# First block's mixers: where the convolution taps are emitted, and the order of the output projection's units

## The chip, the cores and the metric

One core of one Trainium2 chip. The metric is the time of one execution on the device in microseconds; several executions are timed, and their median counts. A profile of one execution gives the start and the length of every instruction on the engines: PE (TensorE; PEld is its weight load), DVE (VectorE), ACT (ScalarE), POOL (GpSimd) and the DMA queue of SP (SyncE).

## What is computed

Two transformer blocks over 256 tokens of width 1024. The first has two layers, and the change lies in the mixer of each of them:

```python
proj = h @ w_in + b_in                       # columns: conv | q | k | v | memory query
conv_out = silu(layer_norm(depthwise_conv31(a * sigmoid(gate)) + conv_b))     # 256 channels
diff_out = rms(softmax(s1) @ v - lam * softmax(s2) @ v)                       # 4 heads, 512 wide
mem_out  = softmax(qm @ km.T) @ vm                                            # 4 heads, 256 wide
mixed = concatenate([conv_out, diff_out, mem_out]) @ w_out + b_out
x = layer_norm(ALPHA * x + mixed)
x = layer_norm(ALPHA * x + square(relu(x @ w_up)) @ w_down)
```

A second block (sparse attention, a state-space scan and a gated feed-forward) follows; the change does not touch it.

## The kernel before

All weights lie in HBM as units of 1 MB (128 partitions x 2048 floats). `weight` (L242 to L257) loads a unit with one DMA of SP's queue into a `raw` buffer, of which there are two, and splits it into a rounded part `hi` (ACT, L255) and a rest `lo` (DVE, L256), each in two halves; there are four buffers of `hi` and of `lo`. A raw buffer is free for the next unit's DMA when its `lo` is done. Each product is made of three matmuls, hi·hi, hi·lo and lo·hi (`mm3`, L261 to L263).

`mixer_ops` emits one layer's mixer for two token tiles t of 128 and two head pairs hp. First comes the convolution's input (`conv_in`, leaving `u`), then keys and queries (`chan`, two units each), the scores of the first head pair, the values, and the taps. `conv` is one chain of 31 steps for each of two channel halves c, on DVE, each step reading what the last one wrote:

```python
for j in range(1, 31):
    vec.scalar_tensor_tensor(out=y, in0=u[:, c, j:j + 256], scalar=tap(j), in1=y, op0=OP.mult, op1=OP.add)
```

Then a loop of four steps n goes over d = (0,0), (0,1), (1,0), (1,1), pairs (t, hp). Each step emits the scores of the next pair (`diff_scores`: matmuls L533, the reduction with the relative bias on DVE L540, four exponentials on ACT L519) and the values of this pair (`diff_values`: scaling on ACT L557 and DVE L558, transposes L340, eviction L561, matmuls L565). Step 0 also emits the memory query (`chan` "qm", one unit, 48 matmuls and eviction L495); steps 1 and 3 `diff_norm` (ACT L573 and L579); steps 1 and 2 `mem_attention` (matmuls L589, DVE L593, ACT L599 and L603); step 2 `mem_values` (transposes L615, eviction L617, matmuls L621, and a split into `mixT` at L345 and L346). Steps 0 and 1 emit `conv_out` (transposes L629, DVE L633 to L641, ACT L635 and L640). Parts of the second block's position bias, `position_bias_part`, are spread over the steps: loads `rel` through SP, ACT L877 and L882, matmuls L880.

The mixers' results lie side by side in `mixT`: columns 0 and 1 the convolution, 2 to 5 the four difference heads, 6 and 7 the memory. The output projection takes four units of two columns each, in the order of the list `order`: unit 0 is the convolution, 1 and 2 the difference heads, 3 the memory. In `layer`, `downs` (L279 to L291) adds them up in two accumulators `acc` (PSUM) for each token tile: for the units in front of the last both column halves c together, then the last unit. One unit of one token tile is 12 matmuls, so 48 a tile and 96 a layer. The accumulation makes their order fixed. `row` buffers, two in all, hold rows that are broadcast to all partitions: the convolution's norm (`self.cln`), then b_out, and the layer norm's gain and offset (ln_g, ln_b), loaded through SP (L369). Scores and memory scores use the same four `acc` buffers.

The order on each engine is not the order of the code. The tile framework puts the instructions into the engines' queues ahead of time, by its own estimate of when each is ready; among those that it holds ready, the one emitted first goes first. An instruction that is emitted late but needs little can therefore run early. Each engine then runs its queue strictly in that order.

Of the kernel before, what the change touches and what calls it, by code (L numbers as in the profile page):

```python
# [198 lines left out]
class Kernel:  # L199
# [455 lines left out]
    def mixer_ops(self, l):  # L655
        nc, vec, gp, a = self.nc, self.nc.vector, self.nc.gpsimd, self.a
        self.cln = self.row(a["lay"], 1536 * l)
        self.v = [self.b1.tile([128, 512], F32, name="v", tag=f"v{t}") for t in range(NT)]
        self.kT = self.new("kq", [128, 4, S])
        self.qT = self.new("kq", [128, 4, S])  # L660
        self.qmT = self.b1.tile([128, 2, S], F32, name="qmT")
        self.conv_in(l)
        eighth = lambda c: self.scaled[:, c:c + 1]
        self.chan(l, "k", 8, self.kT, lambda c: self.col("b_in", c), 1.0)
        self.chan(l, "q", 4, self.qT, eighth, 0.125)
        if l == 0:
            self.position_bias()
        self.mixT = self.pair("mh", [128, KD, S])
        d = [(0, 0), (0, 1), (1, 0), (1, 1)]
        st = self.diff_scores(l, 0, 0)  # L670
        vs = [self.weight("v", l, h) for h in range(2)]
        for t in range(NT):
            self.values(l, vs, t)
        self.conv(l, 0)
        self.conv(l, 1)
        for n, (t, hp) in enumerate(d):
            if n < 3:
                nxt = self.diff_scores(l, *d[n + 1])
            self.diff_values(l, t, hp, *st)
            st = nxt  # L680
            if n == 0:
                self.chan(l, "qm", 16, self.qmT, eighth, 0.125)
            if n < 2:
                self.conv_out(l, n)
            if n % 2:
                self.diff_norm(l, t)
            if 0 < n < 3:
                self.mem_attention(l, n - 1)
            if n == 2:
                self.mem_values(l)  # L690
            for m in range((0, 2, 3, 4)[n], (2, 3, 4, 8)[n]):
                self.position_bias_part(8 * l + m)
        bo = self.row(a["b_out"], D * l)
        for t in range(NT):
            vec.scalar_tensor_tensor(out=self.x[t], in0=self.x[t], scalar=ALPHA, in1=bo, op0=OP.mult, op1=OP.add)
        order = (0, 3, 1, 2)
        ws = [self.weight("out", l, i) for i in order]
        return order, ws

# [704 lines left out]
```

## Time and profile before

| | us |
|---|---|
| median of 3 runs | 1275.21 |
| lowest, highest | 1273.62, 1282.3 |
| profiled execution | 1279.33 |
| its span, first to last instruction | 1277.6 |

Times in rows are counted from the start of the span, so 1.73 us of the profiled execution lie outside of it. In a timeline row stand the start, the length, the engine, the line, the operation, what it writes and reads, the shapes and how many were merged; brackets give the idle time of the engine just before and what ended it. The mixer of the first layer runs from about 43 to 167 us, that of the second from about 360 to 476 us.

### The profile page before, as it was taken

To read this page: it belongs to the slowest core of one execution; us is meant where nothing else is said; L and a number is where in the kernel's file an instruction comes from. 1 tells how busy PE (TensorE), PEld (TensorE's weight loads), DVE (VectorE), ACT (ScalarE), POOL (GpSimd) and SP (SyncE) were. 2 spreads that over 40 slices of the span, in tenths; PEclk is the share of its full clock that TensorE was granted. 3 is DMA by queue.
4 is the path that set the end of the run, shared out by engine and by line. 5 is a ranking of instruction groups with operands and counts; after the bars stand their busy time and mean duration, and the time that the engine had idled before them with its cause. 6 is when DMAs were issued, how large, how long until landed. Compare 5 with 4: busy or idle time off the path is not lost.

```text
span 1277.6 us, 20408 instructions
## 1 busy us (share of the span) xinstructions
PE 1203.1 (94%) x8031; PEld 1064.6 (83%) x8031; DVE 966.1 (76%) x1741; ACT 662.8 (52%) x1082; POOL 65.2 (5%) x75
## 2 busy tenths in 40 slices
PE   6997989999999899999988899999999999999997
PEld 5886679899888568998877788789999968899996
DVE  5898577777789667787768995389999987655553
ACT  4546754444353875444335577555555634544441
POOL 2100000000000000000001000000111110000000
PEclk9998999999999899999989999999999999999999
DMA  8733567777561556777735344165454534554450
GB/s 310 263 138 122 191 217 261 253 294 278 198 239 67 190 189 242 273 272 256 279 105 192 120 161 167 70 243 190 164 185 185 185 110 159 198 199 180 183 198 33
DMA packets 53425, 247.81 MB, mean 194 GB/s; under 512 B 5277, under 2 KB 17597, under 8 KB 30545
## 3 DMA queue, kind: packets, MB, share of 16 engines
q1 hardware_dynamic: 52256, 243.22, 53.0%
q0 software_dynamic: 1072, 3.28, 0.8%
q8 instruction: 63, 1.03, 0.3%
q14 instruction: 34, 0.27, 0.1%
HBM read 241.06 MB, written 6.47 MB: 194 GB/s over the span
## 4 chain that ended last, share of the span: by engine, by line
PE 59%; DVE 18%; DMA 11%; ACT 7%; issue 4%; POOL 0%; SPq 0%; DVEq 0%; ACTq 0%; POOLq 0%
PE mm L263 11%; PE mm L262 11%; PE mm L261 11%; PE acc L263 7%; PE acc L261 7%; PE acc L262 6%; DVE lo L256 6%; DMA raw<-in_wts 6%; DVE cy L512 3%; DMA s<-in_ada 3%; ACT hi L255 3%; PE tr L340 1%; DVE t L779 1%; DMA rel<-reld 1%; DVE mask L1015 1%
## 5 line engine op out<-in xcount | busy, mean ns | idle before, releaser
L255 ACT ACTIVATE hi<-raw 128x1024 fp32r<-128x1024 f32 (+1 forms) x367 | 367.3, 1025 | 376.0 <-DMA raw<-in_wts 169.8
L256 DVE TENSOR_TENSOR lo<-raw,hi 128x1024 fp32r<-128x1024 f32 (+1 forms) x367 | 431.6, 1185 | 153.5 <-ACT hi L255 152.9
L261 PE MATMUL mm<-xT,hi 128*128 128x256 f32 x992 | 282.8, 285 | 2.6 <-DVE zs L1147 1.5
L263 PE MATMUL mm<-xT,lo 128*128 128x256 f32 x992 | 282.5, 285 | 0.0
L262 PE MATMUL mm<-xT,hi 128*128 128x256 f32 x992 | 282.1, 284 | 0.0
L261 PEld LDWEIGHTS mm<-xT,hi 128*128 128x128 f32 x992 | 191.8, 193 | 5.1 <-DVE zs L1147 1.7
L262 PEld LDWEIGHTS mm<-xT,hi 128*128 128x128 f32 x992 | 191.7, 193 | 0.8
L263 PEld LDWEIGHTS mm<-xT,lo 128*128 128x128 f32 x992 | 191.9, 193 | 0.2
L261 PE MATMUL acc<-hi,mh 128*128 128x512 f32 x320 | 127.8, 399 | 5.3 <-ACT mh L599 5.3
L262 PE MATMUL acc<-lo,mh 128*128 128x512 f32 x320 | 126.4, 395 | 0.0
L263 PE MATMUL acc<-hi,mh 128*128 128x512 f32 x320 | 125.9, 394 | 0.0
L262 PE MATMUL mm<-lo,xT 128*128 128x256 f32 (+1 forms) x288 | 85.7, 298 | 2.1 <-DVE lo L256 2.1
L263 PE MATMUL mm<-hi,xT 128*128 128x256 f32 (+1 forms) x288 | 86.4, 300 | 1.2 <-DVE xT L346 1.2
L261 PE MATMUL mm<-hi,xT 128*128 128x256 f32 (+1 forms) x288 | 87.1, 302 | 0.1
L779 DVE SCALAR_TENSOR_TENSOR t<-s,silu_c,t 128x512 f32<-128x512 f32 x84 | 62.9, 749 | 30.8 <-DMA s<-in_ada 30.3
L263 PE MATMUL mm<-h,lo 128*128 128x256 f32 x288 | 80.6, 280 | 0.0
L261 PE MATMUL mm<-h,hi 128*128 128x256 f32 x288 | 80.3, 279 | 0.0
L262 PE MATMUL mm<-h,hi 128*128 128x256 f32 x288 | 80.3, 279 | 0.0
L261 PEld LDWEIGHTS acc<-hi,mh 128*128 128x128 f32 x320 | 60.9, 190 | 18.7 <-ACT mh L599 6.1
L263 PEld LDWEIGHTS acc<-hi,mh 128*128 128x128 f32 x320 | 60.5, 189 | 13.8 <-issue 1.4
L262 PEld LDWEIGHTS acc<-lo,mh 128*128 128x128 f32 x320 | 60.7, 190 | 12.5 <-issue 1.1
L261 PEld LDWEIGHTS mm<-hi,xT 128*128 128x128 f32 x288 | 55.5, 193 | 5.2 <-issue 1.8
(382 smaller groups left out, 2220.7 us busy)
## 6 DMA issues: line engine op xcount, KB each, us to landing
raw<-in_wts SPq DMA_DIRECT2D x174, 1024.0 KB
s<-in_ada SPq DMA_DIRECT2D x48, 512.0 KB
rel<-reld SPq DMA_DIRECT2D x64, 64.0 KB
bias<-bo SPq DMA_DIRECT2D x16, 256.0 KB
bias<-bias SPq DMA_DIRECT2D x8, 512.0 KB
cr<-cumd SPq DMA_DIRECT2D x8, 512.0 KB
mh<-in_wts SPq DMA_DIRECT2D x3, 1024.0 KB
row<-in_ln_g SPq DMA_DIRECT2D x4, 512.0 KB
```

The costliest lines, as they stand in the source:

```text
L255: nc.scalar.activation(h[:, s], raw[:, s], AF.Copy)
L256: (lo_on or nc.vector).tensor_tensor(out=l[:, s], in0=raw[:, s], in1=h[:, s].bitcast(F32), op=OP.subtract)
L261: t.matmul(out=out, lhsT=l[0], rhs=r[0], start=start, stop=False)
L262: t.matmul(out=out, lhsT=l[0], rhs=r[1], start=False, stop=False)
L263: t.matmul(out=out, lhsT=l[1], rhs=r[0], start=False, stop=stop)
L340: self.nc.tensor.transpose(out=p[:, i, :], in_=x[:, i * 128:i * 128 + 128], identity=self.ident)
L512: vec.scalar_tensor_tensor(out=y, in0=u[:, c, j:j + 256], scalar=tap(j), in1=y, op0=OP.mult, op1=OP.add)
L779: vec.scalar_tensor_tensor(out=acc, in0=w[:, k, :], scalar=s, in1=acc, op0=OP.mult, op1=OP.add)
L1015: vec.scalar_tensor_tensor(out=isc, in0=rl[:, i, :], scalar=self.widx[:, t, h:h + 1], op0=OP.mult, op1=OP.add, in1=self.nadm[:, t, :] if h ...
```

## The change

The two calls of `conv` move from ahead of the loop into its steps 0 and 1, behind that step's `diff_values` (and in step 0 behind the memory query). `conv_out` moves from steps 0 and 1 to steps 2 and 3. The output projection adds memory, difference heads 0 and 1, convolution, difference heads 2 and 3, where it was convolution, memory, heads 0 and 1, heads 2 and 3. No instruction is added or removed.

```diff
         for t in range(NT):
             self.values(l, vs, t)
-        self.conv(l, 0)
-        self.conv(l, 1)
         for n, (t, hp) in enumerate(d):
             if n < 3:
                 nxt = self.diff_scores(l, *d[n + 1])
@@
             if n == 0:
                 self.chan(l, "qm", 16, self.qmT, eighth, 0.125)
             if n < 2:
-                self.conv_out(l, n)
+                self.conv(l, n)
+            else:
+                self.conv_out(l, n - 2)
             if n % 2:
                 self.diff_norm(l, t)
@@
-        order = (0, 3, 1, 2)
+        order = (3, 1, 0, 2)
         ws = [self.weight("out", l, i) for i in order]
```

## Rows read from the trace of the kernel before

**Rows 1.** The page: busy time, share of the span and number of instructions by engine; the chain that ended last, by engine.

```profile
PE 1203.1 (94%) x8031; PEld 1064.6 (83%) x8031; DVE 966.1 (76%) x1741; ACT 662.8 (52%) x1082; POOL 65.2 (5%) x75
PE 59%; DVE 18%; DMA 11%; ACT 7%; issue 4%; POOL 0%; SPq 0%; DVEq 0%; ACTq 0%; POOLq 0%
```

**Rows 2.** Busy time by stretch: the stretch, its length, then busy us (and instructions) of PE, PEld, DVE, ACT, POOL, the granted TensorE clock, the DMA engines' busy share, GB/s. Five stretches of the first layer, two of the second's mixer.

```profile
84.00:97.50 13.50, 11.99 (x56) 9.33 (x54) 13.22 (x50) 4.54 (x13) 0.00 (x0) 1.00 0.00 1
97.50:106.50 9.00, 4.57 (x31) 3.83 (x32) 9.00 (x32) 3.46 (x11) 0.74 (x3) 0.80 0.07 23
121.30:143.00 21.70, 18.14 (x104) 12.51 (x103) 9.50 (x30) 18.24 (x52) 1.57 (x2) 0.84 0.58 188
143.00:167.20 24.20, 22.83 (x133) 16.64 (x131) 17.75 (x30) 16.69 (x30) 2.01 (x2) 1.00 0.68 230
200.00:360.00 160.00, 159.99 (x991) 144.37 (x990) 126.72 (x159) 69.87 (x83) 0.92 (x1) 1.00 0.70 252
...
410.00:420.00 10.00, 9.94 (x78) 8.53 (x78) 10.00 (x27) 3.86 (x12) 0.55 (x1) 1.00 0.34 123
431.00:445.00 14.00, 10.14 (x49) 6.73 (x46) 6.74 (x25) 11.59 (x41) 1.56 (x2) 0.76 0.69 242
```

**Rows 3.** Timeline of DVE, first layer: the longest merged group of taps, the memory query's two `lo` halves, and the scaling of x by ALPHA, which is emitted behind the whole loop.

```profile
77.04 8.00 DVE L512 SCALAR_TENSOR_TENSOR cy<-u,cols,cy 128x256 f32<-128x256 f32 x20
...
102.26 2.35 DVE L256 TENSOR_TENSOR lo<-raw,hi 128x1024 fp32r<-128x1024 f32 x2
...
108.81 2.35 DVE L695 SCALAR_TENSOR_TENSOR x<-x,row 128x1024 f32<-128x1024 f32 x2
```

**Rows 4.** What SP's queue waited for (total us, times, longest us): the first row from 60 to 180 us, the second from 370 to 480 us. Then, from the timeline of SP in the first layer, the load of the layer norm's offset.

```profile
SPq L249 <- DVE lo L256: 42.9, 6, 27.1
...
SPq L249 <- DVE lo L256: 40.9, 6, 24.8
...
127.64 0.92 SPq L369 DMA_DIRECT2D row<-in_ln_b  x1
```

**Rows 5.** Timeline of PE, first layer: the waits behind the values, a group of value matmuls at full clock, and the wait ahead of the second token tile's first output unit.

```profile
102.02 0.41 PE L340 MATMUL tr<-ident,t 128*128 128x128 f32 x2 [2.69 <-DVE ds L517]
...
104.60 2.08 PE L565 MATMUL mm<-v,t 128*128 128x128 f32 x8 [1.73 <-ACT t L561]
...
118.58 1.16 PE L565 MATMUL mm<-v,t 128*128 128x128 f32 x8
...
128.35 0.79 PE L261 MATMUL acc<-hi,mh 128*128 128x512 f32 x1 [2.38 <-ACT mh L599]
```

**Rows 6.** The chain that ended last, first layer: start, length and kind of two of the memory query's matmuls, one before and one after the clock rose.

```profile
106.68 0.21 PE mm L261
...
113.55 0.12 PE mm L262
```

**Rows 7.** Timeline of ACT, first layer: the wait for the second pair's scores, the eviction of the memory query, and the rounding of the memory's result into `mixT`.

```profile
101.99 0.51 ACT L519 ACTIVATE s<-s,ds 128x256 f32<-128x256 f32 x1 [9.24 <-DVE ds L517]
...
113.83 0.84 ACT L495 ACTIVATE qmT<-mm,scaled 128x256 f32<-128x256 f32 x2 [1.82 <-PE mm L263]
...
142.02 0.60 ACT L345 ACTIVATE mh<-mm 128x512 fp32r<-128x512 f32 x1 [0.38 <-PE mm L621]
```

**Rows 8.** Groups by line and form (count, busy us, mean ns, idle before): taps from 85 to 105 us; exponentials with their sums, scalings and the rounding of the convolution's result from 113.8 to 142.7 us; exponentials with their sums from 419.7 to 452.7 us; from 121.3 to 142.9 us the output projection's hi·hi matmuls, one in three of its matmuls.

```profile
L512 DVE SCALAR_TENSOR_TENSOR cy<-u,cols,cy 128x256 f32<-128x256 f32 x26 | 11.0, 480 | 0.0
...
L519 ACT ACTIVATE s<-s,ds 128x256 f32<-128x256 f32 x4 | 2.0, 514 | 0.0
L557 ACT ACTIVATE t<-s,ds 128x256 f32<-128x256 f32 x4 | 1.8, 513 | 0.0
...
L519 ACT ACTIVATION_READ_ACCUMULATOR s<-s,ds 128x1 f32 x4 | 0.8, 208 | 0.0
L640 ACT ACTIVATE mh<-tr 128x256 fp32r<-128x256 f32 x2 | 0.8, 383 | 0.0
...
L519 ACT ACTIVATE s<-s,ds 128x256 f32<-128x256 f32 x8 | 4.0, 505 | 0.0
L519 ACT ACTIVATION_READ_ACCUMULATOR s<-s,ds 128x1 f32 x8 | 1.6, 199 | 0.0
...
L261 PE MATMUL acc<-hi,mh 128*128 128x512 f32 x8 | 4.3, 537 | 2.4 <-ACT mh L599 2.4
```

**Rows 9.** Timeline of PE, first layer: the first and the last of 24 output matmuls that follow each other without another instruction between them.

```profile
145.58 0.39 PE L262 MATMUL acc<-lo,mh 128*128 128x512 f32 x1
...
150.82 0.39 PE L261 MATMUL acc<-hi,mh 128*128 128x512 f32 x1
```

**Rows 10.** Timeline of ACT, second layer: the eviction of the first pair's transposes, the second pair's first exponential, the eviction of the memory query, and the rounding of the memory's result.

```profile
411.58 0.60 ACT L561 ACTIVATE t<-tr 128x512 f32<-128x512 f32 x1 [6.04 <-PE tr L340]
...
415.42 0.51 ACT L519 ACTIVATE s<-s,ds 128x256 f32<-128x256 f32 x1 [3.25 <-DVE ds L517]
...
419.73 0.84 ACT L495 ACTIVATE qmT<-mm,scaled 128x256 f32<-128x256 f32 x2
...
452.06 0.60 ACT L345 ACTIVATE mh<-mm 128x512 fp32r<-128x512 f32 x1 [0.50 <-PE mm L621]
```

**Rows 11.** Timeline of PE: the longest wait of the second layer's mixer, and the wait for the position bias ahead of the first layer's feed-forward.

```profile
438.68 0.80 PE L261 MATMUL acc<-hi,mh 128*128 128x512 f32 x1 [2.87 <-ACT mh L599]
...
172.27 0.52 PE L880 MATMUL tr<-step,bd 128*64 128x256 bf16 x6 [3.04 <-ACT step L877]
```

## The prediction

> **What bounds the kernel now.** The page first: PE is busy for 94% of the span and is 59% of the chain that ended last [rows 1], so time is won where PE waits or runs slowly. The stretches say where. In the feed-forward, from 200 to 360 us, PE is busy for 159.99 of 160 us; in the first layer's mixer, from 97.5 to 106.5 us, for 4.57 of 9, at a granted clock of 0.80, while DVE is busy throughout [rows 2]. So I read DVE's queue next. In the 20 us from 85 to 105 us, 26 taps take 11.0 us [rows 8], and behind them, at 102.26 us, stand the `lo` halves of the memory query's unit [rows 3]. Three engines wait for that. SP's queue waits 27.1 us on a `lo`, its longest [rows 4], and the DMA share falls to 0.00 [rows 2]. ACT waits 9.24 us for the second pair's scores, which DVE takes up only behind taps [rows 7]. PE waits 2.69 and 1.73 us, then does eight value matmuls in 2.08 us that take 1.16 us at full clock [rows 5], and the memory query's first matmuls at 0.21 us each, later ones at 0.12 [rows 6].
>
> From the memory query's eviction (113.83 us) to its attention's result in `mixT` (142.02 + 0.60 us) the bound is another one: ACT is busy for 18.24 of 21.7 us, PE has a clock of 0.84 [rows 2, 7]. PE gets through this with 24 of the 96 output matmuls, the convolution's: 8 of each of three kinds, of which the row shows one [rows 8]. From there PE is busy for 22.83 of 24.2 us to the end of the mixer [rows 2].
>
> The second layer has the same order but no hole at the same place: from 410 to 420 us PE is busy for 9.94 of 10 us [rows 2], though SP waits 24.8 us [rows 4] and ACT 6.04 and 3.25 us [rows 10]. Its loss lies from 431 to 445 us, PE 10.14 of 14 us at 0.76 [rows 2], the longest wait being 2.87 us for ACT's memory exponentials [rows 11].
>
> **What the planner will do.** Position in the code is a rank, not a time: the scaling of x, emitted behind the whole loop, ran at 108.81 us [rows 3]. Taps that fill DVE while keys and queries are made, such as the 20 from 77.04 us [rows 3], stay where they are, since nothing ahead of them in rank is ready. What moves are about 26 taps of the first layer, 11.0 us [rows 8], and about as many of the second: they fall behind the second pair's scores, the first pair's values and the memory query's `lo`. They need 11 us of DVE elsewhere, and there is room: from 121.3 to 143 us DVE works 9.5 of 21.7 us, from 431 to 445 us 6.74 of 14 [rows 2]. Their cost is then nothing; were that room gone, 11 us. Two chains of taps can still cut in between single DVE steps, one tap of 0.48 us at a time.
>
> **First layer, ahead of the memory query.** PE's waits of 2.69 + 1.73 = 4.4 us go [rows 5]. With them goes the slow clock behind them: 2.08 - 1.16 = 0.9 us on the value matmuls [rows 5], and on the query's 48 matmuls (113.83 - 106.68) - 48 x 0.12 = 1.4 us [rows 6, 7]. Sum 6.7 us. What is late next is PE itself, since the values fill it up to there.
>
> **Second layer, same place.** PE is full, so nothing: 0.
>
> **The stretch bound by ACT.** Exponentials that can run while ACT now waits leave it. First layer: the last pair's, 2.0 + 0.8 = 2.8 us; one of the two pairs of scalings, 1.8 / 2 = 0.9; and the rounding of the convolution's result, 0.8, which moves to its end [rows 8]. Sum 4.5 us. Second layer: two pairs' exponentials, 4.0 + 1.6 = 5.6 us [rows 8], and by the first layer's rows again 0.9 + 0.8: 7.3 us, of which the waits of 6.04 + 3.25 us can hold all [rows 10]. Unknown is how much other ACT work (rounding of output units, position bias) drops into the place; it may eat all of it (0), or the two gains may be as computed (11.8). I take the computed ones, being nearest to the waits seen.
>
> **The order of the units.** This speaks against the change. With the memory's unit first, no output matmul can run before the memory's result is there. The 24 that now fill the stretch come after it: 24 x (150.82 - 145.58) / 23 = 5.5 us a layer [rows 8, 9], as nothing covers them there. The convolution, third now, is wanted 24 matmuls, or 5.5 us, after the result, so the later taps and `conv_out` should not be waited for. Bounds for a wait on it: none, or the 2.69 us that a transpose waited for DVE [rows 5]; I take none.
>
> **Other queues.** The moved steps issue no DMA, but `conv_out` frees the row buffer of `cln`, into which ln_b goes, at 127.64 us now [rows 4]. Issued later, it holds back weight loads behind it in SP's queue; between nothing and the load's own 0.92 us a layer, and I take nothing, as the query's raw buffer comes free some 15 us earlier. POOL, 1.57 us busy of 21.7 [rows 2], takes `conv_out`'s small power without loss.
>
> **Sum.** First layer 6.7 + 4.5 - 5.5 = 5.7 us; second 7.3 - 5.5 = 1.8 us; together 7.5 us. The profiled execution, 1279.33 us, would become 1271.8; it lies 4.1 us over the median of the runs, so the median goes from 1275.2 to about **1268 us**. What follows, the feed-forward and the second block, is unchanged and should only shift.
>
> **Rivals.**
> *More is won.* The memory's result comes so early that PE never lacks work. Then every loss in the two mixers goes: 6.7 us, the 2.38 us wait [rows 5] and, with `rel` loads early in SP's queue, the 3.04 us for the position bias [rows 11], 12.1 us; and in the second layer 14 - 10.14 = 3.9 us [rows 2]. 16 us: 1259. For it: ACT's 9.24 us of waiting [rows 7] could hold three pairs. Against: the filler is gone.
>
> *Nothing moves in the stretch.* ACT stays as full as it is, with other work: 6.7 - 5.5 - 5.5 = -4.3 us, 1279.5. For it: ACT's busy share there is set by everything queued on it, not by scores alone.
>
> *Slower: the filler was worth more than its matmuls.* The place is PE between the memory query and the memory's result. Without the convolution's 24 matmuls PE waits longer for ACT, and the clock falls: after the waits of rows 5 it was 0.80, and the lost clock cost 0.9 + 1.4 = 2.3 us. If the memory's result comes less than 5.5 us earlier in both layers, this decides: 2 x (5.5 + 2.3) = 15.6 us lost, 1291. For it: from 431 to 445 us PE already lacks 3.9 of 14 us at a clock of 0.76 [rows 2]. Against: the 6.7 us ahead of it are nearly sure.
> [...]
>
> *The change doesn't do what it says.* The planner, holding the taps ready, still puts them ahead of the query's `lo`. Then only the order of the units acts: 2 x 5.5 = 11 us lost, 1286.
>
> **From cases to numbers.** Chances: forecast 0.42, more is won 0.23, nothing moves 0.18, slower 0.12, not as said 0.05. A measurement of this kernel can tell about 1%, 12.8 us, from no change. Faster than that (under 1262.5) are nearly all of the first rival and the lower tail of the forecast: 0.27. Slower (over 1288) is the third rival: 0.12. The rest, 0.61, lies within. Leaving out the third rival and the outer tails of the others, the range is 1256 to 1283.
>
> **What would show it.** In the profile after: the query's `lo` near 90 us instead of 102.26 and SP's wait on it near 12 us; PE without waits behind the values; the query's eviction near 107 us; the memory's result near 131 and 445 us; its first output matmuls right behind, none before; the mixers' ends 6 and 8 us earlier than now. Wrong it is if ACT is still full from the query to the memory's result at the old length, if PE's clock there lies well under 0.76, or if the output matmuls wait for the convolution.

## The result, and the profile after

The changed kernel is slower: 1297.84 us in the median of four runs, against 1278.68 for the kernel before in the same series, ratio 1.0123 [1.0082, 1.0165], some 16 us. The forecast was 7.5 us faster. The ratio leaves out the slowest execution, 1303.49 us, which lies 1.5% above the fastest of the four; the profile is of that one, so the argument leans also on two later runs in which one layer alone is changed, and which repeat its mixers (the second to 0.1 us, the first 2.9 us shorter).

Three rows of each layer measure a mixer: the first output of the convolution's input in the first layer, or the last in the second (L487), the memory's result (L345), the last add of the layer norm (L650). In the changed kernel (start, length, engine, line):

```profile
55.76 0.39 ACT L487 ACTIVATE u<-tr 128x256 f32<-128x256 f32 x1 [1.60 <-PE tr L340]
...
140.42 0.60 ACT L345 ACTIVATE mh<-mm 128x512 fp32r<-128x512 f32 x1 [0.38 <-PE mm L621]
...
174.29 0.69 DVE L650 TENSOR_TENSOR x<-acc,x 128x512 f32<-128x512 f32 x1
...
383.83 0.39 ACT L487 ACTIVATE u<-tr 128x256 f32<-128x256 f32 x1 [1.14 <-PE tr L340]
...
494.14 0.69 DVE L650 TENSOR_TENSOR x<-acc,x 128x512 f32<-128x512 f32 x1
```

The same rows of the kernel before, with those of the memory's result in [rows 7, 10]:

```profile
56.27 0.39 ACT L487 ACTIVATE u<-tr 128x256 f32<-128x256 f32 x1 [1.38 <-PE tr L340]
...
167.86 0.68 DVE L650 TENSOR_TENSOR x<-acc,x 128x512 f32<-128x512 f32 x1
...
378.29 0.39 ACT L487 ACTIVATE u<-tr 128x256 f32<-128x256 f32 x1 [0.93 <-PE tr L340]
...
477.81 0.69 DVE L650 TENSOR_TENSOR x<-acc,x 128x512 f32<-128x512 f32 x1 [0.53 <-PE acc L263]
```

From the first to the last of these the first mixer grew from 111.6 to 118.5 us, the second from 99.5 to 110.3. The first layer holds the smaller part although the hole ahead of its query was filled as forecast. The query's `lo` runs at 80 us, not 102.26 [rows 3]; PE is full behind the values; the query is evicted at 107.74, not 113.83 [rows 7]. The timeline of DVE and ACT, and the stretch behind the values (columns as in rows 2), both after:

```profile
79.78 1.22 DVE L256 TENSOR_TENSOR lo<-raw,hi 128x1024 fp32r<-128x1024 f32 x1
...
107.74 0.84 ACT L495 ACTIVATE qmT<-mm,scaled 128x256 f32<-128x256 f32 x2 [2.08 <-PE mm L263]
```

```profile
97.50:107.50 10.00, 9.98 (x83) 8.73 (x81) 10.00 (x29) 4.48 (x13) 0.00 (x0) 1.00 0.07 23
```

Then it is lost. The stretches from the query's eviction to the memory's result, before and after, first and second layer (columns as in rows 2), and two parts of them after:

```profile
113.83:142.02 28.19, 24.51 (x158) 16.96 (x157) 14.77 (x44) 23.54 (x66) 1.57 (x2) 0.88 0.54 170
419.73:452.06 32.33, 26.19 (x164) 17.08 (x165) 19.32 (x63) 28.07 (x78) 1.56 (x2) 0.89 0.48 161
```

```profile
107.74:140.42 32.68, 23.07 (x130) 15.02 (x129) 23.00 (x63) 27.82 (x75) 1.77 (x4) 0.69 0.50 172
119.00:134.00 15.00, 8.53 (x40) 6.01 (x40) 9.08 (x24) 13.94 (x43) 0.55 (x1) 0.50 0.58 209
424.70:460.71 36.01, 23.63 (x130) 15.13 (x130) 21.79 (x60) 28.06 (x75) 1.56 (x2) 0.67 0.51 167
434.00:454.00 20.00, 11.03 (x48) 7.60 (x48) 11.24 (x32) 17.69 (x50) 1.56 (x2) 0.51 0.51 173
```

The stretches are 4.5 and 3.7 us longer, not 4.5 and 7.3 shorter. In the first layer ACT's work grew from 23.54 to 27.82 us: the query moved ahead, and what ACT had done in front of it now falls behind it. Groups of ACT before and after, from 113.83 to 142.02 and from 107.74 to 140.42 us:

```profile
L519 ACT ACTIVATE s<-s,ds 128x256 f32<-128x256 f32 x4 | 2.0, 514 | 0.0
L255 ACT ACTIVATE hi<-raw 128x1024 fp32r<-128x1024 f32 x1 | 1.1, 1060 | 0.0
```

```profile
L255 ACT ACTIVATE hi<-raw 128x1024 fp32r<-128x1024 f32 x4 | 4.0, 1048 | 1.5 <-DMA raw<-in_wts 1.5
L519 ACT ACTIVATE s<-s,ds 128x256 f32<-128x256 f32 x8 | 3.9, 497 | 0.0
```

And the order is bad. What the memory's first exponentials read is done by 115.4 us (L594 on DVE); they run at 124.44. The second pair's exponentials, at 112.02, were still ahead of that time; from 115.4 on ACT rounds an output unit, which itself waits for its load, and does the third pair's exponentials and scalings and some smaller steps before it takes the memory:

```profile
112.02 0.51 ACT L519 ACTIVATE s<-s,ds 128x256 f32<-128x256 f32 x1
...
115.22 0.16 DVE L594 TENSOR_SCALAR ma<-ma 128x4 f32<-128x4 f32 x1
...
117.53 2.00 ACT L255 ACTIVATE hi<-raw 128x1024 fp32r<-128x1024 f32 x2 [1.53 <-DMA raw<-in_wts]
119.44 0.49 ACT L519 ACTIVATE s<-s,ds 128x256 f32<-128x256 f32 x1
...
124.44 0.46 ACT L599 ACTIVATE mh<-acc,ma 128x256 f32<-128x256 f32 x1
```

Meanwhile PE has nothing to fill with: 8.53 of 15 us busy, at a granted clock of 0.50.

### The profile page after: what moved, and what is told of

It reads as the page before. It is cut to its first block, busy times and chain, and to the rows that moved or that the text cites. A ratio compares the mean times of both kernels' runs of the same rounds, so it can differ in the third digit from the quotient of the medians.

```text
span 1301.7 us, 20416 instructions
## 1 busy us (share of the span) xinstructions
PE 1215.7 (93%) x8031; PEld 1070.6 (82%) x8031; DVE 969.4 (74%) x1741; ACT 664.3 (51%) x1082; POOL 65.3 (5%) x75
## 4 chain that ended last, share of the span: by engine, by line
PE 50%; DVE 21%; DMA 17%; ACT 7%; issue 4%; POOL 1%; SPq 0%; DVEq 0%; ACTq 0%; POOLq 0%
DMA raw<-in_wts 10%; PE mm L261 10%; PE mm L263 10%; PE mm L262 10%; DVE lo L256 8%; DMA s<-in_ada 5%; PE acc L262 4%; PE acc L263 4%; PE acc L261 4%; ACT hi L255 3%; DVE t L779 2%; PE tr L340 2%; DMA rel<-reld 2%; DVE mask L1015 1%; PE mm L1107 1%
## 5 line engine op out<-in xcount | busy, mean ns | idle before, releaser
L261 PE MATMUL mm<-xT,hi 128*128 128x256 f32 x992 | 282.5, 285 | 1.8 <-ACT xs L1125 1.0
L263 PE MATMUL mm<-xT,lo 128*128 128x256 f32 x992 | 282.1, 284 | 0.0
L261 PEld LDWEIGHTS mm<-xT,hi 128*128 128x128 f32 x992 | 191.4, 193 | 4.5 <-ACT xs L1125 1.9
L263 PEld LDWEIGHTS mm<-xT,lo 128*128 128x128 f32 x992 | 191.3, 193 | 0.0
L261 PE MATMUL acc<-hi,mh 128*128 128x512 f32 x320 | 126.2, 394 | 2.3 <-ACT mh L345 2.3
L263 PE MATMUL acc<-hi,mh 128*128 128x512 f32 x320 | 126.9, 396 | 0.4 <-DVE mh L346 0.3
L261 PE MATMUL mm<-hi,xT 128*128 128x256 f32 (+1 forms) x288 | 87.9, 305 | 1.4 <-ACT kmT L468 1.4
L263 PE MATMUL mm<-hi,xT 128*128 128x256 f32 (+1 forms) x288 | 86.7, 301 | 0.5 <-DVE xT L346 0.5
L779 DVE SCALAR_TENSOR_TENSOR t<-s,silu_c,t 128x512 f32<-128x512 f32 x84 | 62.7, 747 | 31.8 <-DMA s<-in_ada 31.3
L261 PE MATMUL mm<-h,hi 128*128 128x256 f32 x288 | 80.7, 280 | 0.0
L263 PE MATMUL mm<-h,lo 128*128 128x256 f32 x288 | 80.4, 279 | 0.0
L261 PEld LDWEIGHTS acc<-hi,mh 128*128 128x128 f32 x320 | 60.6, 189 | 14.7 <-ACT mh L345 2.7
L263 PEld LDWEIGHTS acc<-hi,mh 128*128 128x128 f32 x320 | 60.4, 189 | 14.6 <-DVE mh L346 1.3
L261 PEld LDWEIGHTS mm<-hi,xT 128*128 128x128 f32 x288 | 56.2, 195 | 6.4 <-ACT kmT L468 2.3
```

Of the source, the lines that this page charges most:

```text
L261: t.matmul(out=out, lhsT=l[0], rhs=r[0], start=start, stop=False)
L263: t.matmul(out=out, lhsT=l[1], rhs=r[0], start=False, stop=stop)
L779: vec.scalar_tensor_tensor(out=acc, in0=w[:, k, :], scalar=s, in1=acc, op0=OP.mult, op1=OP.add)
```

## Experiments

Theory A: the order of the units costs the time, since nothing fills the stretch any more. Rival B: the moved taps and `conv_out` cost it, by a new wait in SP's queue and late results. Two more came up on the way: A2, the memory's result is held up by the order in which ACT takes its work, and C, the loss is scatter set off by any disturbance.

One table for most runs. For each layer: us from L487 to the memory's result, output matmuls that PE did between query and result, us from the result to the last L650 (the tail). They come from the same three rows in each run's trace, and a count of `acc` matmuls by L261 to L263.

| run | ratio to before, 95% | first layer | second layer |
|---|---|---|---|
| before | 1 | 85.8, 24, 25.8 | 73.8, 22, 25.8 |
| the change | 1.0123 [1.0082, 1.0165] | 84.7, 0, 33.9 | 76.9, 0, 33.4 |
| e1 order alone | 1.0126 [1.0086, 1.0166] | 85.7, 0, 31.3 | 75.6, 0, 31.6 |
| e2 taps and conv_out alone | 1.0108 [1.0080, 1.0136] | 83.5, 10, 31.4 | 77.5, 12, 30.7 |
| e3 the same, conv_out a step earlier | 1.0093 [1.0059, 1.0127] | 87.9, 18, 27.9 | 75.0, 18, 28.0 |
| e4 query first | 1.0083 [1.0052, 1.0115] | 88.7, 24, 26.2 | 79.5, 22, 26.4 |
| e5 second layer only | 1.0115 [1.0076, 1.0153] | 88.2, 24, 25.6 | 77.0, 0, 33.4 |
| e6 first layer only | 1.0022 [0.9995, 1.0049] | 82.1, 0, 33.5 | 75.1, 22, 26.1 |
| e7 memory first | 1.0068 [1.0043, 1.0093] | 74.4, 0, 34.1 | 71.9, 0, 35.5 |
| e9 other order | 1.0091 [1.0065, 1.0118] | 81.6, 24, 31.5 | 76.2, 24, 31.3 |
| e10 before, memory first | 0.9977 [0.9951, 1.0004] | 83.6, 24, 28.8 | 69.5, 23, 25.9 |
| e11 memory first, first layer only | 0.9995 [0.9970, 1.0020] | 75.1, 0, 34.0 | 75.0, 22, 26.2 |

Layers with the same code show the scatter: the way to the result differs by up to 2.6 us, the tail by 0.4.

**The two edits apart.** Order alone is a change of one line; the other run is the changed kernel with that line undone.

```diff
-        order = (0, 3, 1, 2)
+        order = (3, 1, 0, 2)
```

> The kernel before with only the output projection's units in the new order (memory, heads 0 and 1, convolution, heads 2 and 3); taps and conv_out stay where they were. Theory A (the order costs the time: no output matmul is left to fill the stretch from the memory query to the memory's result, PE falls to 0.50 there, and the output units free their buffers late, so that the feed-forward's first weights are late): slower by 16 to 25 us, since the early memory query, which gave 6 us in the changed kernel, is missing here; granted clock near 0.50 in the first layer from the query to the memory's result; up weights' first rounding some 8 us later than in the kernel before. Rival B (the moved taps and conv_out cost it, by a new wait in SP's queue and late results): 0 to 5 us slower here. My own pricing of the order, 5.5 us a layer for 24 matmuls and nothing else: 11 us slower.

> The changed kernel with the units in the old order (convolution, memory, heads 0 and 1, heads 2 and 3): only taps and conv_out are moved. Theory A: 0 to 8 us faster than the kernel before; the memory query's lo near 80 us in the first layer, PE full behind the values. Rival B: 12 to 18 us slower, as the changed kernel. What speaks for a part of B even here: the convolution, first in the order, is now done late (its result stood at 143 to 147 us in the changed kernel), so that its 24 matmuls again fill nothing ahead of the memory's result; then the two edits overlap, each alone costs 10 us or more, and the sum of both alone is larger than the change.

1298.86 and 1296.82 us against 1282.63: each costs about as much as both. So theory A missed the second run, rival B the first, and this is the overlap named in the second expectation. In part both take the same thing away: with the memory first nothing can fill; with a late convolution its matmuls come too late to fill (10 and 12 of 24 still do). But the 14 and 10 matmuls that are missing in the second run against before make some 3.2 and 2.3 us, an estimate from the 0.23 us each of [rows 9], and its tails grew by 5.6 and 4.9; what makes up the rest is not shown.

The first run also prices the filler and the clock on the way to the result, since there ACT has as much to do as before (23.94 and 28.15 us busy). Its stretches from the query to the result, first and second layer:

```profile
111.39:141.05 29.66, 20.41 (x139) 14.23 (x138) 14.94 (x44) 23.94 (x66) 1.57 (x2) 0.77 0.51 169
425.96:459.68 33.72, 21.82 (x138) 14.23 (x139) 19.41 (x63) 28.15 (x77) 1.56 (x2) 0.80 0.45 154
```

With no filler and a clock of 0.77 and 0.80 they are 1.5 and 1.4 us longer than before. The clock near 0.50 that theory A expected over this stretch did not come from the order alone.

The run that follows is the second one with `conv_out` a step earlier:

```diff
-            else:
-                self.conv_out(l, n - 2)
+            if 0 < n < 3:
+                self.conv_out(l, n - 1)
```

> Taps moved as in the changed kernel, conv_out one step earlier than there (steps 1 and 2), units in the old order. Theory A: as the run with the taps alone, or up to 5 us faster, since the convolution's matmuls come earlier and can fill. If the late conv_out is what costs (the overlap of both edits): clearly faster than the run with taps and conv_out as changed in the old order, by 3 to 8 us. Rival B by its wait in SP's queue: as slow as that run.

1293.83 us. With the results one step earlier 18 matmuls fill, and the tail falls to 28 us. Against e2 the time is 3 us better, but the intervals overlap; the tails tell them apart. The tails are not all of its loss: its profile is 18.9 us longer than that of before, of which 7.7 lie in the two mixers and most of the rest in the feed-forwards and the second block, whose code no run here edits.

**The early query alone.**

```diff
+        self.chan(l, "qm", 16, self.qmT, eighth, 0.125)
         self.conv(l, 0)
         self.conv(l, 1)
@@
-            if n == 0:
-                self.chan(l, "qm", 16, self.qmT, eighth, 0.125)
```

> The kernel before with the memory query emitted ahead of the two convolution chains; taps otherwise, conv_out and order untouched. This takes from the change only what gave time in its trace: an early lo of the memory query. Theory A: the gain ahead of the query, 4 to 7 us in the first layer, is kept to the end: 3 to 7 us faster than the kernel before. If the gain is eaten by the stretch bound by ACT, as in the changed kernel: 0 to 2 us. Rival B says nothing against it.

1294.19 us, 11 us slower: both theories missed. The query is evicted at 101.72 us, 12 us earlier than before, but the result comes at 144.52, later. The fill and the tail are as before; all of the loss in the mixers is on the way to the result. An early query buys nothing by itself. In its trace DVE still does taps up to 105 us, and the memory's first exponentials, ready to run at 114.83, run at 119.32 behind the third pair's scores; how much of the 11 us each of these makes was not tested.

**The layers apart.** The whole change under `if l == 1`, or under `if l == 0`.

> The change in the second layer alone; the first layer, and with it everything up to about 360 us, is that of the kernel before. What each of the five other profiles shows: they lose some 5 us at the first layer's mixer or at the end of its feed-forward, 3 to 11 us in the second layer's mixer, about 4 us in the second feed-forward, 2 to 5 us at the start of the second block. Theory A, places: a mixer loses by its own change, so the profile agrees with the kernel before to within 2 us up to 360 us, the second mixer loses 8 to 11 us and the second feed-forward 4: 11 to 15 us slower. Rival C (any disturbance ahead of it throws the later stretches out of a favourable phase, so that most is lost away from the edit): the second mixer loses 5 or less and the sum is below 8 us. If the end of the first feed-forward, where the code is untouched, stalls here too, that part is scatter between executions and belongs to no edit.

> The change in the first layer alone; the second layer's mixer is that of the kernel before. Theory A: the first layer loses about 6 us up to the second layer's convolution input, the second mixer keeps its length of 99.5 us (from the last convolution input to the last add of the layer norm), and the sum with the second-layer run is the whole change: 3 to 7 us slower. Rival C: the second mixer is longer by 3 us or more although nothing in it is edited, and the sum of the two single-layer runs is larger than the change by 5 us or more.

1298.04 and 1286.07 us against 1282.55: 15.5 us and 3.5 us by medians, 14.7 and 2.8 by the ratios. Together 17.5, as the change within its interval. So the loss is additive by layer as far as the intervals tell, rival C falls, and most of the loss lies in the second layer, where there was no hole ahead of the query to fill. The single-layer traces repeat the mixers:

```profile
384.43 0.39 ACT L487 ACTIVATE u<-tr 128x256 f32<-128x256 f32 x1 [1.29 <-PE tr L340]
...
494.77 0.69 DVE L650 TENSOR_TENSOR x<-acc,x 128x512 f32<-128x512 f32 x1
```

```profile
57.28 0.39 ACT L487 ACTIVATE u<-tr 128x256 f32<-128x256 f32 x1 [1.59 <-PE tr L340]
...
172.93 0.69 DVE L650 TENSOR_TENSOR x<-acc,x 128x512 f32<-128x512 f32 x1
...
381.60 0.39 ACT L487 ACTIVATE u<-tr 128x256 f32<-128x256 f32 x1 [1.25 <-PE tr L340]
...
482.81 0.69 DVE L650 TENSOR_TENSOR x<-acc,x 128x512 f32<-128x512 f32 x1 [0.38 <-PE acc L263]
```

Second layer changed alone: second mixer 110.3 us, as in the change. First layer changed alone: first mixer 115.7, second 101.2. The first run also starts its second layer 6 us later than the profile of before, with the same code up to there; that is scatter between executions.

**The order on ACT.**

```diff
         for n, (t, hp) in enumerate(d):
+            if 0 < n < 3:
+                self.mem_attention(l, n - 1)
+            if n == 2:
+                self.mem_values(l)
             if n < 3:
                 nxt = self.diff_scores(l, *d[n + 1])
@@
-            if 0 < n < 3:
-                self.mem_attention(l, n - 1)
-            if n == 2:
-                self.mem_values(l)
```

> The changed kernel with the memory's attention and values emitted at the head of their steps, ahead of the next pair's scores, not behind them. In the trace of the changed kernel the memory's first exponentials run at 124.4 us, although what they read is done by 115.3: ACT works through the scores of two pairs and the rounding of an output unit in front of them. Theory A2 (the memory's result is held up by ACT's order, since the early scores go ahead of it): first-layer memory result at 130 to 134 us, not 140.4, and 5 to 12 us faster than the changed kernel (1286 to 1293 against 1298). If the result is bound by ACT's work as a whole or by the slow matmuls, whatever the order: result within 3 us of 140, time as the changed kernel.

1290.71 us, 7 us better than the changed kernel, as theory A2 said (the intervals of the two ratios overlap a little; the memory's result tells them apart). The memory's exponentials now stand ahead of the second token tile's scores:

```profile
108.80 0.47 ACT L599 ACTIVATE mh<-acc,ma 128x256 f32<-128x256 f32 x1
...
112.71 0.49 ACT L519 ACTIVATE s<-s,ds 128x256 f32<-128x256 f32 x1
...
129.75 0.60 ACT L345 ACTIVATE mh<-mm 128x512 fp32r<-128x512 f32 x1 [0.38 <-PE mm L621]
```

The result comes 10.7 us earlier in the first layer and 11.6 in the second (449.11 against 460.71; 5 counted from L487). The edit moves the memory ahead on PE and DVE as well: its exponentials are ready 4.0 us after the query, not 7.6, and then wait for ACT 0.3 us, not 9.1. Some 8 us against before are left. By the profiles the first mixer is 3.1 us shorter than before and the second 7.8 longer, through the tails of 34.1 and 35.5 us; more lies in the first feed-forward (3.8 us longer) and the second block (4.9 us).

**The filler and the clock.** The changed kernel with `order = (1, 2, 3, 0)`:

> The changed kernel with the units in the order heads 0 and 1, heads 2 and 3, memory, convolution: the first token tile's difference heads are normalised by about 124 us, so 24 output matmuls can again run ahead of the memory's result at 140. Theory A (the missing filler, with the clock at 0.50 that comes with it, is what costs): the stretch from 119 to 134 us at a higher clock than 0.50, the mixers 4 to 7 us shorter than in the changed kernel, the time 8 to 14 us better: 1284 to 1290, and at best that of the kernel before. If the filler is worth nothing: as the changed kernel within 3 us.

1293.41 us, 4 us better than the changed kernel, half of the least that theory A expected. Set beside e7, this tells the clock from the order. Stretches from the query to the result of e9, then of e7:

```profile
107.34:139.06 31.72, 23.90 (x154) 16.89 (x155) 23.13 (x63) 27.78 (x75) 1.77 (x4) 0.89 0.52 176
420.38:455.70 35.32, 26.20 (x154) 18.36 (x154) 22.20 (x61) 27.94 (x76) 1.56 (x2) 0.81 0.47 156
```

```profile
104.51:129.75 25.24, 18.75 (x107) 12.22 (x106) 15.35 (x47) 21.74 (x66) 1.22 (x3) 0.80 0.46 155
418.15:449.11 30.96, 19.13 (x107) 11.59 (x106) 17.25 (x48) 23.81 (x69) 1.02 (x1) 0.72 0.46 144
```

With 24 matmuls to fill, e9 has the clock back (0.89 and 0.81, from 0.69 and 0.67), and the stretch is shorter by 1.0 and 0.7 us. With nothing to fill and a clock of 0.80 and 0.72, e7 is shorter by 7.4 and 5.1. So the order, above all on ACT, sets most of this length, and the clock, together with the filler that brings it, is worth about a microsecond, as in e1. The filler of e9 did not shorten the tail to 26. The convolution, last in its order, is waited for only 0.41 us in each layer. A longer wait is that for the second token tile's difference heads, which DVE scales (L576) behind the first tile's layer norm; the profile puts it down to DVE's next step, L333:

```profile
150.14 1.09 PE L340 MATMUL tr<-ident,t 128*128 128x128 f32 x4 [2.40 <-DVE cl L333]
```

The second layer has the same wait of 2.40 us, and behind it PE runs slower: the output matmuls just ahead of the wait take 0.39 and 0.40 us each, the first ones behind it 0.63 to 0.80 us. Over the tails of the kernel before and of the changed kernel the granted clock is 1.00.

Two runs meant to measure the clock directly, with matmuls that nothing reads, were ill made:

```diff
         po = self.mm()
+        for _ in range(16):
+            pe.matmul(out=po[:, 0, :], lhsT=self.qmT[:, 0, 0:128], rhs=self.qmT[:, 1, :], start=True, stop=True)
```

> The changed kernel with 16 extra matmuls a layer on the memory query, into the accumulator that the memory's values use later; nothing reads them, and the output is the same. They can run from the query on, in any wait of PE: work that fills and does nothing. If the slow clock by itself is what the lost filler cost (PE's matmuls in the stretch take twice as long, 2.42 against 1.13 us for eight memory scores): granted clock above 0.7 between the query and the memory's result, that stretch shorter by 2 to 4 us a layer, 4 to 8 us better than the changed kernel. If it is the filler's own matmuls, now to be done later (5.5 us a layer), and the late buffers: no gain, 0 to 3 us slower than the changed kernel, even where the clock rises. If the stretch is bound by ACT's order alone: no gain either, with the memory's result at 140 and 461 us as before.

> The changed kernel with 18 extra matmuls a layer on the memory query, six at the end of each of the first three steps, into a transposes' accumulator; nothing reads them. They are ready from the query on and rank behind the step's own work, so they run where PE waits, between 108 and 134 us. If the slow clock is a large part of the loss: granted clock in 119 to 134 us from 0.50 to above 0.75, eight memory scores at 1.2 us in place of 2.4, memory's result 2 us or more earlier in both layers, 3 to 8 us better than the changed kernel. If it is ACT's order and the matmuls that come later: clock up, result within 1 us, time within 3 us of the changed kernel or slower.

1306.40 and 1310.50 us, ratios 1.0168 [1.0126, 1.0211] and 1.0238 [1.0208, 1.0269]. The dead matmuls did not run in PE's waits: in the first run they stood at 130 to 138 us, in front of the memory's values, in the second twelve records at 128 us, as one block of 4.84 us. The memory's result came later, counted from L487 by 2.9 and 3.3 us in the first run and by 7.8 and 4.8 in the second. They show that PE is on the path there; they say nothing on the clock.

**The load in front of the bias.** In the changed kernel SP's queue waits for the position bias, from the unit issued at 82.55 us to 101.38:

```profile
SPq L875 <- ACT step L877: 21.5, 3, 18.4
SPq L249 <- DVE lo L256: 17.0, 4, 5.4
```

```diff
-            self.ring(self.b1, mh=3, row=2, kq=2, s=2, t2=4, t1=3, step=2, rel=2, bo=1)
+            self.ring(self.b1, mh=3, row=2, kq=2, s=2, t2=4, t1=3, step=3, rel=4, bo=1)
```

> The changed kernel with four buffers for the loads of the position bias where there were two, and three for their steps. In the changed kernel a load of the position bias waits for such a buffer from 82.9 to 101.4 us and holds the next unit's load behind it in SP's queue. If this new wait, in the place of the removed one, is what costs: the wait gone, the second value-side loads some 15 us earlier, 4 us or more better than the changed kernel. If the order of the units is what costs: as the changed kernel within 3 us.

1300.78 us, ratio 1.0133 [1.0100, 1.0166], as the changed kernel. But the wait stayed (its longest 18.5 us), so the run doesn't clear it. What speaks against it as the cause is e7, which has the same wait (the bias loads go at 98 us there) and the shortest way to the result.

**Versions that might beat both.** The memory at the head of its steps in the kernel before (e10), the same in the first layer of the changed kernel with the second layer as before (e11), and e10 with the convolution's and the memory's unit applied to both token tiles ahead of the others (e16); and the changed kernel with the memory's unit applied to both tiles first (e15), which tests the late buffers (the new argument `part` of `downs` picks the units; its own lines are left out):

```diff
-        for t in range(NT):
-            acc = [self.acc(), self.acc()]
-            self.downs(acc, [(self.mixT, (2 * i, 2 * i + 1)) for i in order], ws, t)
-            self.close(t, acc, None, g, b, xT)
+        ops = [(self.mixT, (2 * i, 2 * i + 1)) for i in order]
+        accs = [[self.acc(), self.acc()] for _ in range(NT)]
+        for t in range(NT):
+            self.downs(accs[t], ops, ws, t, part=(0,))
+        for t in range(NT):
+            self.downs(accs[t], ops, ws, t, part=(1, 2))
+            self.close(t, accs[t], None, g, b, xT)
```

> The kernel before with nothing but the memory's attention and values emitted at the head of their steps; taps, conv_out and the order of the units as they were. From the changed kernel this took 7 us. If the memory's result is late here by the same rule, it comes earlier in both layers (142.0 to below 137, 452 to below 447), and with the convolution's filler kept the time is 3 to 10 us better than the kernel before, a version that beats both. If the kernel before already runs the memory as early as its query lets it (its first exponentials start 5 us after the query), no gain: within 3 us, and the earlier memory may only push the scores back: up to 5 us slower.

> First layer: the change with the memory at the head of its steps. Second layer: the kernel before. The run with the memory first in both layers ended the first mixer at 163.8 us against 167.9 to 171.5 with the code of before, and then lost it in the first feed-forward (194.5 against 190.7 to 192.5 us). By places: first mixer 3 to 5 us shorter than before, second mixer 99 to 102 us: the sum 0 to 5 us faster than the kernel before. If the feed-forward's weights, not the mixer's end, set the pace: no difference, within 2 us.

> The changed kernel with the output projection's first unit (the memory) applied to both token tiles before the other units, same sums in the same order for each tile. The buffer of the memory's unit is then free some 6 us behind the memory's result and not 18. If the late buffers are the cause of the late first weights: the first rounding of the feed-forward's weights 8 us or more earlier in both layers (165.5 and some 485 us in the changed kernel), PE's hole at the second feed-forward's start (6.5 of 10 us busy) mostly gone, second feed-forward 196 us and not 199.6, 4 to 8 us better than the changed kernel. If the weights are late for another reason (ACT's or SP's order): within 2 us.

> The kernel before with the memory first in its steps, and with the convolution's and then the memory's unit applied to both token tiles before the difference heads' units. The memory first made the second mixer 95.4 us long (99.5 to 101.2 before) and the feed-forward behind it 201.6 (195.7 to 196.7), so that nothing was left. If that loss is weights that wait for buffers: second feed-forward back at 196 to 198, the time 4 to 8 us faster than the kernel before, the only version to beat it. If the weights' stream as a whole sets the pace: within 3 us of it.

e10: 1281.39 us; e11: 1284.45, against 1284.10. Neither differs from the kernel before. e10 shortens the second mixer to 95.4 us, and the second feed-forward (from the last L650 to the row of the last two L652) grows from 195.7 to 201.6; e11 shortens the first mixer by 2 to 5 us and nothing of it is left at the end. e16: 1.0032 [0.9999, 1.0065], second feed-forward 201.8. e15: 1301.80 us, 1.0176 [1.0128, 1.0223]. In e15 the second feed-forward's first weights are rounded 12 us earlier than in the changed kernel, and it takes 199.7 us against 199.6. The first rounding in e15, then in the changed kernel:

```profile
473.23 1.06 ACT L255 ACTIVATE hi<-raw 128x1024 fp32r<-128x1024 f32 x1 [1.65 <-PE acc L263]
```

```profile
484.93 1.06 ACT L255 ACTIVATE hi<-raw 128x1024 fp32r<-128x1024 f32 x1 [1.27 <-PE acc L263]
```

So the late buffer is real and is not what costs. None of these beats the kernel before.

## Why the prediction was wrong

**Ahead of the query: right.** Gains of 6.7 and 0 us were forecast; from L487 to the query's eviction the first layer went from 57.6 to 52.0 us, 5.6 gained, the second from 41.4 to 40.9.

**The stretch bound by ACT: the step that failed.** 4.5 and 7.3 us were to leave it; it grew by 4.5 and 3.7, a miss of 9 and 11 us. I counted exponentials that *could* run in ACT's waits ahead of the query. They did not leave the stretch: the query itself moved ahead of them in the first layer (four exponentials in the stretch before, eight after), and in the second eight stand there in both. My lower bound, that other ACT work eats the gain, was zero; nothing excluded a loss, and the stretch begins at a point that I was moving myself. Nor did I ask in which order ACT would take its work: the scores that come earlier go ahead of the memory's exponentials, which alone decide when the output matmuls begin. e7 shows it: with the memory ahead of the scores, 7.4 and 5.1 us of the stretch are gone.

**The order of the units: right in kind and nearly in size.** 5.5 us a layer were forecast. With the order alone (e1) the tail grew by 31.3 - 25.8 = 5.5 and 31.6 - 25.8 = 5.8 us.

**The convolution not waited for: right to 0.4 us, but the tail grew further.** With the late `conv_out` as well the tail is 33.4 to 33.9, another 2 us. PE's waits for the convolution, in the changed kernel's two tails:

```profile
146.37 0.41 PE L340 MATMUL tr<-ident,t 128*128 128x128 f32 x2 [0.39 <-DVE t L636]
...
466.66 0.41 PE L340 MATMUL tr<-ident,t 128*128 128x128 f32 x2 [0.39 <-DVE t L636]
```

More than half of the 2 us is work: PE is busy for 31.5 us in these tails, for 30.1 and 30.5 in those of e1, with the transposes of `conv_out` (L629, L340) now among it. I had no term for work of the convolution that falls behind the result.

**What follows should only shift: wrong in the second layer.** The second feed-forward took 199.6 us and, with the second layer changed alone, 202.5, against 195.7 to 196.7 where that layer is untouched: some 5 us. But it is no fixed part of the change: in e7 and e13, with the second layer changed too, it took 195.2 and 194.9 us. In the changed kernel PE lacks work at its start, 6.49 of the 10 us that begin at about the last L650, against 8.87 before (after, then before):

```profile
493.80:503.80 10.00, 6.49 (x52) 6.28 (x51) 8.79 (x17) 4.50 (x5) 0.92 (x1) 0.93 0.58 218
```

```profile
478.29:488.29 10.00, 8.87 (x68) 7.84 (x67) 9.93 (x19) 6.75 (x9) 0.93 (x1) 1.00 0.85 296
```

Why is open: the buffer of the first unit is excluded by e15, the weights' stream as a whole (e10, e16) is not. The second block did not only shift either: 607.2 us from the last L652 to the end, against 603.3 before; it took 603 to 610 us in the profiles of the table's runs, so part of this is scatter.

**Other queues: not told apart.** The offset's load [rows 4] went at 145.34 us, 18 later, and SP got a new wait of 18.4 us in place of the 27.1 on the query's `lo`; no run takes either away alone.

**The sum by place**, with the single-layer runs and, for the unchanged second mixer, e11: first mixer (118.5 + 115.7) / 2 against (111.6 + 113.9) / 2, 4.4 us; second mixer 110.3 against (99.5 + 101.2 + 101.2) / 3, 9.7 us; second feed-forward 5 us. Together 19, against 16 [10, 21] by the ratio; the second block is not in it.

**The slower rival** came nearest. It had the right condition (the result less than 5.5 us earlier: it came 1.1 us earlier and 3.1 later, counted from L487), the right place and nearly the right time, 1291 against 1275.21 x 1.0123 = 1290.9. Of its two terms the filler holds; the clock fell as it said, here to 0.50, but with the filler it cost about 1 us a layer on the way to the result (e9), not 2.3. The rest of the stretch was ACT's order, and the second feed-forward's 5 us were not in its sum at all, so that its time came out is partly luck. In the stretches of 15 and 20 us above the granted clock was 0.50 and 0.51. A low clock is one matter, its cost another: PE still idles there for 6.5 and 9.0 us, waiting for other engines, and getting clock and filler back brought the result forward by about 1 us only (e9; e1 agrees). I gave this rival 0.12, because the gain ahead of the query seemed sure. It came, and the stretch behind the query took most of it back: counted from L487 the result was only 1.1 us earlier.

## What to carry to other kernels

Ask of an operation that becomes ready earlier what it will stand in front of: in a strict queue an early arrival that nobody waits for delays the one on which the next stage depends. Here the memory's first exponentials waited 9.1 us for ACT, behind an output unit's rounding and the third pair's scores, and 0.3 us where they stood ahead (e7). Follow that one chain (here the memory's exponentials) to its end before counting any gain ahead of it. And work that can run at any time has its worth where nothing else can: moving it behind the wait cost its full length here, 5.5 us of matmuls a layer by the forecast, 5.5 and 5.8 us in e1.

## What the runs showed of the hardware

A load of the same 1 MB unit, issued at 112.19 us in the changed kernel and at 112.23 in e15 behind the same queue, reached ACT at 117.53 and at 121.98 us. ACT waited 1.53 and 5.95 us for it, and in the changed kernel the memory's exponentials, whose inputs were done by 115.4 us, stood behind it in ACT's queue and ran at 124.44. In e15:

```profile
121.98 2.00 ACT L255 ACTIVATE hi<-raw 128x1024 fp32r<-128x1024 f32 x2 [5.95 <-DMA raw<-in_wts]
```

Part of the scatter between executions of one kernel, 1275 to 1295 us for the kernel before in the longest series, may come from such places; that was not tested.
